# Second MLP product in pairs of output sets: half steps in turn, block sums on GpSimd, two evictions by ScalarE

## The chip, the cores and the metric

One core of a Trainium2 chip runs the whole kernel. TensorE multiplies, VectorE (DVE), ScalarE (ACT) and GpSimd (POOL) work on tiles in SBUF and, apart from GpSimd, in the PSUM banks that TensorE writes; SyncE (SP) issues nearly all DMAs. The metric is the device time of one execution in microseconds: lower is better.

## The reference, cut to what matters

```python
def reference(x, p, ...):                       # x: 1 x 1024 x 1024, float32
    h = x
    for i in range(2):                          # two layers
        hn = rmsnorm(h, norm1[i])
        ...                                     # pooling mixer and windowed attention
        h = h + concat([pool_out, attn_out]) @ w_out[i]
        hn = rmsnorm(h, norm2[i])
        h = h + square(relu(hn @ w_up[i])) @ w_down[i]     # 1024 -> 4096 -> 1024
        gate = sigmoid(rmsnorm(h, norm3[i]) @ w_gate[i])
        h = h + gate * (p[i] @ w_ple[i])
    return rmsnorm(h, final_norm)
```

Everything is float32. The change is in the two products of the MLP, above all in the second, `@ w_down`, and at its two ends.

## The kernel before, in words

**Transposed activations, split operands.** Activations lie with the features on the partitions and the 1024 positions in the columns, as eight tiles of 128 x 1024; `hf` is a half of 512 columns. Each operand of a product is split into a rounded high part and a low part (ScalarE writes the high part, DVE subtracts it to get the low one), and three matmuls of 128x512 (high x high, high x low, low x high) stand for one float32 product.

**Seven products.** Both MLP products treat a pair of 128-row weight columns, a pair of k tiles and the two column halves as 2 x 2 blocks, and take seven block products, `P1` to `P7`, for eight. A *set* is one pair of output tiles over some k positions: a position is a pair of k tiles, and a product over n positions is 3n matmuls (`products7`). The products of a set run in the order P1, P7, P6, P2, P5, P4, P3. P1, P6, P5 and P3 add up one on the other in one PSUM bank, X; P7 and P4 in Z; P2 stands alone in Y. X banks come from a pool of three ("mm"), Y and Z banks from pools of two ("s", "e"). After each product `close` reads its bank out, so the next product into the same bank has to wait for that reading.

**The weights' side** is class `Seven`: `load` brings a set's weights by SP, `sums` makes four sums of blocks on GpSimd (L280 to L287), and `make` writes one split piece per product, `u0p`/`d0p` in layer 0 and `u1p`/`d1p` in layer 1 (ScalarE L299, DVE L301). `lead` sets how far ahead: loading, sums and pieces start so many products before they are used.

**The first product (up, `Up`)** has 16 sets of four positions. ScalarE copies P1, P7 and P6 out of PSUM into `y1` and `y2` (L1131 to L1136), DVE adds P2, P5 and P4 or takes P3 with the relu (L1139 to L1154), ScalarE squares (L1157). The squared set is one *position* of the second product. `sums` (L1162) writes its seven blocks to DRAM, `x_d`: three as they are, four as differences that DVE makes into `ys` (L1172 to L1178).

**The second product (down, `Down`)** gets these blocks back: `x_back` (L1187) is one DMA of 256 KB, a high part by ScalarE (L1192) and a low part by DVE (L1194), all in one tile `wP`. Position i serves all four output pairs t. `STEPS` lists the sets as (t, first position, last): three short ones with 3, 2 and 1 positions, thirteen of four positions, and three short ones with 3, 2 and 1 at the end, so that the four output pairs run one position apart. `close` (L1205) adds every product with one DVE instruction from PSUM into the residual `acc` (L1210). When an output pair has all 16 positions, `rest` splits it into `g` (L504, L506) and squares it for the third norm (`norm3.add`, L424 on ScalarE, L426 on GpSimd).

**What sets the order.** Each engine has one queue and runs it in order; SP's queue of DMA issues too. The program is written by a planner (`Clock`): it keeps an estimate of TensorE's time, and a generator's `yield 900.0` puts the next instruction into its queue 900 ns later by that estimate. It knows no queue's real backlog. `ck.need` and `Seven.take` only see to it that a piece has been put into its queues before its product. All big tiles come from one pool of 49 buffers of 4 KB a partition.

## Time and profile before

| | us |
|---|---|
| median of 3 runs | 2370.72 (2370.68 to 2378.85) |
| the profiled execution, its own time | 2371.51 |
| its span in the trace | 2369.7 |
| TensorE busy | 2299.1 (97%) |
| DVE busy | 1711.4 (72%) |
| ScalarE busy | 1007.9 (43%) |
| GpSimd busy | 713.5 (30%) |
| matmuls | 11088 |

In layer 0 the first MLP product runs from 422.8 to 741.5 us of the span and the second from there to 1067.0; in layer 1 from 1587.2 to 1905.9 and to 2231.7. Busy shares are means over the whole program; what a change is worth is read from the places where TensorE stands still, and there from what it waited for. The granted clock of TensorE stands in the tables as a share of its full 2.4 GHz: 0.50 is 1.2 GHz.

### The profile page before, as it was taken

The page shows a single profiled execution, that of the slowest core. Times are in us where ns is not written, and L with a number is a line of the kernel's source. Part 1 is how long each engine was busy: PE and PEld are TensorE (multiplying, and loading weights), DVE is VectorE, ACT ScalarE, POOL GpSimd, SP SyncE. Part 2 cuts the span into 40 slices and gives each one's busy share as a digit, 9 for nine tenths or more (in the row PEclk, how much of TensorE's full clock was granted, in tenths as well). Part 3 has the DMA queues.
Part 4 walks back from the last instruction along what each step waited for, and adds up shares of the span by engine and source line. Part 5 has one row for each costly group of instructions (what it writes and reads, how often), then busy time and mean ns, then how long its engine had stood idle before and what let it go on. Part 6 is the DMA issues. An engine that isn't in the chain of part 4 may idle for free.

```text
span 2369.7 us, 30964 instructions
## 1 busy us (share of the span) xinstructions
PE 2299.1 (97%) x11088; PEld 1850.5 (78%) x11088; DVE 1711.4 (72%) x2888; ACT 1007.9 (43%) x2161; POOL 713.5 (30%) x562
## 2 busy tenths in 40 slices
PE   8999999999999999989999999999999989999898
PEld 6767778788887788877887767887888868888788
DVE  7555667787778888886565466677777798888845
ACT  5244533443335344444324344434433354443545
POOL 5111126323332433342221122253333233332422
PEclk9999999999999999999999999999999999999999
DMA  5011133255448555521120111333444485553214
GB/s 178 19 46 19 38 90 107 67 165 158 155 150 285 160 158 158 149 67 45 55 63 19 37 37 38 90 119 103 154 156 156 155 286 152 158 157 107 85 54 134
DMA packets 292401, 268.31 MB, mean 113 GB/s; under 512 B 12092, under 2 KB 223672, under 8 KB 292248
## 3 DMA queue, kind: packets, MB, share of 16 engines
q1 hardware_dynamic: 289656, 262.70, 36.5%
q0 software_dynamic: 2272, 3.61, 0.9%
q8 instruction: 87, 1.43, 0.2%
q14 instruction: 66, 0.54, 0.1%
q10 hardware_dynamic: 320, 0.03, 0.0%
HBM read 193.65 MB, written 72.58 MB: 112 GB/s over the span
## 4 chain that ended last, share of the span: by engine, by line
PE 46%; DVE 4%; ACT 1%; POOL 1%; DMA 1%; issue 1%; SPq 0%; DVEq 0%; ACTq 0%; POOLq 0%
PE X L535 13%; PE Z L535 7%; PE Y L535 3%; PE in L520 3%; PE in L518 3%; PE in L522 3%; PE gt L522 2%; PE gt L520 2%; PE gt L518 2%; PE s L752 1%; PE o L788 1%; DMA wP<-x_d 1%; PE e L774 1%; PE pl L520 1%; PE pl L522 1%
## 5 line engine op out<-in xcount | busy, mean ns | idle before, releaser
L535 PE MATMUL X<-wP,d1p 128*128 128x512 f32 x768 | 186.7, 393 | 15.0 <-DVE acc L1210 14.4
L535 PE MATMUL X<-wP,d0p 128*128 128x512 f32 x768 | 188.7, 396 | 12.8 <-DVE acc L1210 11.9
L535 PE MATMUL X<-xP,u0p 128*128 128x512 f32 x768 | 186.2, 394 | 3.9 <-ACT y L1131 3.9
L535 PE MATMUL X<-xP,u1p 128*128 128x512 f32 x768 | 185.8, 394 | 3.9 <-ACT y L1131 3.9
L1194 DVE TENSOR_TENSOR wP<-wP 128x512 fp32r<-128x512 f32 x224 | 183.4, 821 | 5.1 <-ACT wP L1192 5.1
L535 PEld LDWEIGHTS X<-wP,d1p 128*128 128x128 f32 x768 | 143.4, 188 | 51.0 <-ACT d1p L299 10.2
L535 PEld LDWEIGHTS X<-wP,d0p 128*128 128x128 f32 x768 | 144.6, 190 | 48.9 <-ACT d0p L299 9.1
L535 PEld LDWEIGHTS X<-xP,u0p 128*128 128x128 f32 x768 | 146.2, 191 | 35.3 <-ACT y L1131 4.7
L535 PEld LDWEIGHTS X<-xP,u1p 128*128 128x128 f32 x768 | 145.9, 190 | 35.2 <-ACT y L1131 4.8
L1157 ACT ACTIVATE y<-y 128x1024 f32<-128x1024 f32 x64 | 67.5, 1055 | 221.5 <-DVE y L1154 221.5
L1192 ACT ACTIVATE wP<-wP 128x512 fp32r<-128x512 f32 x224 | 137.9, 620 | 43.7 <-DMA wP<-x_d 43.3
L188 DVE SCALAR_TENSOR_TENSOR wl<-wr,gt,wh 128x128 fp32r<-128x128 f32 (+1 forms) x288 | 118.7, 443 | 38.5 <-ACT wh L194 38.2
L647 POOL TENSOR_TENSOR rot<-rot,s 128x512 f32<-128x512 f32 x48 | 61.5, 1284 | 277.2 <-DVE rot L645 216.2
L1210 DVE TENSOR_TENSOR acc<-acc,X 128x512 f32<-128x512 f32 x152 | 103.5, 682 | 33.7 <-PE X L535 29.9
L765 ACT ACTIVATE sm<-sm,nm 128x128 f32<-128x128 f32 (+1 forms) x192 | 84.5, 442 | 93.3 <-DVE nm L762 93.1
L194 ACT ACTIVATE wh<-wr,gt 128x128 fp32r<-128x128 f32 (+1 forms) x304 | 104.2, 396 | 0.8 <-DMA wr<-in_w_in_dram 0.7
L758 DVE CUSTOM_DVE_ANT_0 sm<-s,cst 128x128 f32<-128x128 f32 (+1 forms) x192 | 58.3, 346 | 52.0 <-PE s L752 52.0
L535 PE MATMUL Z<-xP,u1p 128*128 128x512 f32 x384 | 94.6, 394 | 0.3 <-DVE xP L1009 0.2
L535 PE MATMUL Z<-xP,u0p 128*128 128x512 f32 x384 | 94.4, 394 | 0.3 <-DVE xP L1009 0.2
L535 PE MATMUL Z<-wP,d0p 128*128 128x512 f32 x384 | 93.5, 390 | 0.0
L535 PE MATMUL Z<-wP,d1p 128*128 128x512 f32 x384 | 93.4, 389 | 0.0
L535 PEld LDWEIGHTS Z<-xP,u1p 128*128 128x128 f32 x384 | 72.9, 190 | 16.3 <-DVE xP L1009 0.5
(474 smaller groups left out, 5982.7 us busy)
## 6 DMA issues: line engine op xcount, KB each, us to landing
wP<-x_d SPq DMA_DIRECT2D x224, 256.0 KB, 2.8
x_d<-ys SPq DMA_DIRECT2D x64, 512.0 KB, 3.5
wr<-in_w_in_dram SPq DMA_DIRECT2D x40, 512.0 KB, 3.8
u0r<-in_w_up_dram SPq DMA_DIRECT2D x32, 512.0 KB, 5.3
x_d<-y SPq DMA_DIRECT2D x32, 512.0 KB, 2.8
u1r<-in_w_up_dram SPq DMA_DIRECT2D x32, 512.0 KB, 5.3
d0r<-in_w_down_dram SPq DMA_DIRECT2D x26, 512.0 KB, 5.2
d1r<-in_w_down_dram SPq DMA_DIRECT2D x26, 512.0 KB, 5.8
```

The costliest lines, as they stand in the source:

```text
L188: nc.vector.scalar_tensor_tensor(l[:, k], raw[:, k], gs[k], f(h[:, k]), op0=OP.mult, op1=OP.subtract)
L194: nc.scalar.activation(h[:, k], raw[:, k], AF.Copy, scale=gs[k])
L518: nc.tensor.matmul(p, wh, h[:, cols], start=first and i == 0, stop=False)
L520: nc.tensor.matmul(p, wh, l[:, cols], start=False, stop=False)
L522: nc.tensor.matmul(p, wl, h[:, cols], start=False, stop=last and i == n - 1)
L535: nc.tensor.matmul(p, w[:, a, i], x[:, b], start=first and i == 0 and a == b == 0, stop=i == n - 1 and a == 1, skip_group_check=not first)
L647: nc.gpsimd.tensor_tensor(a, a, tb["s"][:, hs(hf)], op=OP.mult)
L765: nc.scalar.activation(sm[:, i, hh], sm[:, i, hh], AF.Exp, bias=nm[:, j:j + 1], scale=0.125, accum_out=ml[g][:, n, 4 + h:5 + h])
L1157: nc.scalar.activation(y, y, AF.Square)
L1192: nc.scalar.activation(t[:, 0], f(t[:, 1]), AF.Copy)
L1194: nc.vector.tensor_tensor(t[:, 1], f(t[:, 1]), f(t[:, 0]), op=OP.subtract)
L1210: nc.vector.tensor_tensor(a, a, p, op=OP.add)
```

## The change

- **The sets of the second product.** `STEPS` is now (t, first position, number of positions): output pairs 2 and 3 take positions 0 and 1, then the pairs 0 and 1, then 2 and 3, and so on take four positions each, two positions further every time, and pairs 2 and 3 end with positions 14 and 15. There are 18 sets for 19; the matmuls are as many as before. The products of the first two sets, of the last two, and of the last two sets of the first product run in turn, set by set within each product: P1, P1, P7, P7 and so on.
- **Evictions.** P1 and P6 of a down set are copied by ScalarE into a tile `out`, and GpSimd adds them to `acc` 700 ns later by the planner; the other five stay on DVE.
- **The block sums** of `Up.sums` move from DVE to GpSimd, 1400 ns apart.
- **Blocks back.** `x_back` of positions 0 to 3 now starts during the last two up sets, four after each of their seven products (0, 1.4, 15 and 17.5 us after it). Later, two positions come back after each second set of a pair: one at once and one 9.5 us later.
- **Smaller ones.** The kicks of `Seven` go by a product's real length; small sets share a tile (`two`); the last two out-projection products take other PSUM banks; P5 and P4 of the last `combine` come 4500 instead of 900 ns after P6; `norm3` starts 7000 instead of 3000 ns after the last product.

```diff
-STEPS = [(3, 0, 3), (2, 0, 2), (1, 0, 1)] + [(a % 4, a, min(a + 4, 16)) for a in range(16)]
+ORDER = ("P1", "P7", "P6", "P2", "P5", "P4", "P3")
+STEPS = [(2, 0, 2), (3, 0, 2)] + [(2 * (i // 2 % 2) + i % 2, i // 2 * 2, 4) for i in range(14)]
+STEPS += [(2, 14, 2), (3, 14, 2)]
...
             ck.go(xpiece(i, "P6", T2))
-            yield 900.0
+            yield 900.0 if i < 3 else 4500.0
             ck.go(xpiece(i, "P5", T1))
...
-        outs = [(bank(f"po{L}", ("s", "e")[k // 2]), wk(ws[k % 2], range(8)), hs(k // 2)) for k in range(4)]
+        outs = [(bank(f"po{L}", ("mm", "o", "e", "e")[k]), wk(ws[k % 2], range(8)), hs(k // 2)) for k in range(4)]
...
-                sub = nc.vector.tensor_tensor
+                sub = nc.gpsimd.tensor_tensor
...
+                    if P in ("P1", "P6"):
+                        if P == "P1":
+                            self.out = blk("out")
+                        o = self.out[:, hs(n)]
+                        nc.scalar.activation(o, p, AF.Copy)
+                        ck.go(self.later(a, o))
+                        continue
                     nc.vector.tensor_tensor(a, a, p, op=OP.add)
...
+            def later(self, a, o):
+                yield 700.0
+                nc.gpsimd.tensor_tensor(a, a, o, op=OP.add)
...
-                D7.lead(7 * 12 * 225.0, 2700.0)
-                early = [(i, P) for P in ORDER for i in range(3)] + [(3, P) for P in ORDER]
-                for n, (i, P) in enumerate(early):
-                    ck.at(3200.0 + 1150.0 * n, lambda i=i, P=P: ck.go(x_back(i, P)))
+                D7.lead(8 * 12 * 225.0)
+            n = q - len(seq) + 15
+            if n > 0 and n % 2 == 0:
+                for i in range(4):
+                    ck.at((0.0, 1400.0, 15000.0, 17500.0)[i], lambda i=i, P=seq[q][1]: ck.go(x_back(i, P)))
...
-            if k >= 3 and s.a + 4 < 16:
-                ck.go(x_back(s.a + 4, P))
+            if n == 4 and t % 2 and a + 4 < 16:
+                ck.go(x_back(a + 4, P))
+                ck.at(9500.0, lambda i=a + 5, P=P: ck.go(x_back(i, P)))
...
-        norm3.start(3000.0)
+        norm3.start(7000.0)
```

Three places in the engines' queues, by the order of the built programs (layer 0; the same lines stand 20 to 31 further down in the changed file).

**GpSimd and SP at the start of the second product.** Before, GpSimd has only the weights' sums of the short sets there (`d0s`, from the raw weights `d0r`):

```order
L282 TENSOR_TENSOR d0s0_6267<-d0r1_6184 128x256
L285 TENSOR_TENSOR d0s1_6311<-d0s0_6267,d0r0_6182 128x256
L287 TENSOR_TENSOR d0s1_6311<-d0r0_6182,d0s1_6311 128x256
L280 TENSOR_TENSOR d0s0_6429<-d0r0_6365,d0r1_6367 128x128
L282 TENSOR_TENSOR d0s0_6429<-d0r1_6367 128x128
```

Now GpSimd's queue there, of which this is the end, holds sixteen instructions in a row: the block sums `ys` of the last two up sets (6280 and 6281 of position 14, 6331 and 6332 of position 15), the sums of the third down set and the adds of the first pair's P1 and P6:

```order
L1241 TENSOR_TENSOR acc6_0_6296<-acc6_0_6296,out_6318 128x512
L1193 TENSOR_TENSOR ys0_6331<-y2_6007,y1_5962 128x512
L1197 TENSOR_TENSOR ys1_6281<-y2_5986,ys0_6280 128x512
L302 TENSOR_TENSOR d0s0_6320<-d0r1_6235 128x512
L1195 TENSOR_TENSOR ys0_6331<-y1_5962 128x512
L1200 TENSOR_TENSOR ys1_6281<-y2_5986,ys1_6281 128x512
L305 TENSOR_TENSOR d0s1_6363<-d0s0_6320,d0r0_6233 128x512
L1197 TENSOR_TENSOR ys1_6332<-y2_6007,ys0_6331 128x512
L307 TENSOR_TENSOR d0s1_6363<-d0r0_6233,d0s1_6363 128x512
L1241 TENSOR_TENSOR acc5_0_6267<-acc5_0_6267,out_6294 128x512
L1200 TENSOR_TENSOR ys1_6332<-y2_6007,ys1_6332 128x512
L1241 TENSOR_TENSOR acc7_0_6298<-acc7_0_6298,out_6318 128x512
```

And SP's queue now has the writes of those sums in front of blocks of positions 2 and 3 (`x_d0_2`, `x_d0_3`) that the third set uses:

```order
L1198 DMA x_d0_15_3881<-ys0_6331 128x2x512
L1212 DMA wP5_6375<-x_d0_3_3869 128x512
L1202 DMA x_d0_14_3880<-ys1_6281 128x2x512
L1212 DMA wP4_6411<-x_d0_2_3868 128x512
L1202 DMA x_d0_15_3881<-ys1_6332 128x2x512
L1212 DMA wP4_6432<-x_d0_3_3869 128x512
L273 DMA d0r0_6443<-in_w_down_dram 128x8x128
```

What moved: eight sums went from DVE into GpSimd's queue, and the write of the last one stands ahead of the last blocks of the third set.

**ScalarE at the start of the first product.** `t1`, `t2` are the block sums of the last pair of out-projection rows, X0_3894 is the bank of the first set. Before:

```order
L1007 ACTIVATE xP7_3944<-t1_0_3940 128x512
L1007 ACTIVATE xP6_3953<-t2_0_3941 128x512
L1007 ACTIVATE xP5_3960<-t1_0_3940 128x512
L1007 ACTIVATE xP4_3968<-t2_0_3941 128x512
L1131 ACTIVATE y1_3981<-X0_3894 128x512
L1131 ACTIVATE y1_3983<-X0_3895 128x512
```

Now:

```order
L1027 ACTIVATE xP7_3944<-t1_0_3940 128x512
L1027 ACTIVATE xP6_3953<-t2_0_3941 128x512
L1152 ACTIVATE y1_3974<-X0_3894 128x512
L1152 ACTIVATE y1_3976<-X0_3895 128x512
L319 ACTIVATE u0p_3980<-u0s1_3797 128x512
L1027 ACTIVATE xP5_3985<-t1_0_3940 128x512
```

What moved: the two copies that free the X banks stand ahead of P5's and P4's high parts.

**The end of the second product.** Before, on DVE, with X0_8800 the bank of the last set and the row `acc6_0_6240<-...,X0_8800` its P1:

```order
L506 SCALAR_TENSOR_TENSOR g3_4_0L_8687<-acc4_0_6408,gt_104,g3_4_0H_8686 128x512
L301 TENSOR_TENSOR d0p_8762<-d0s0_8709,d0p_8762 128x128
L1210 TENSOR_TENSOR acc5_0_6410<-acc5_0_6410,Z0_8713 128x512
L506 SCALAR_TENSOR_TENSOR g3_5_0L_8689<-acc5_0_6410,gt_104,g3_5_0H_8688 128x512
L178 TENSOR_TENSOR wl27_8708<-wr27_8703,wh27_8707 128x1024
L301 TENSOR_TENSOR d0p_8778<-d0s1_8742,d0p_8778 128x128
L1210 TENSOR_TENSOR acc4_0_6408<-acc4_0_6408,X0_8692 128x512
L506 SCALAR_TENSOR_TENSOR g3_5_0L_8689<-acc5_0_6410,gt_104,g3_5_0H_8688 128x512
L1210 TENSOR_TENSOR acc6_0_6240<-acc6_0_6240,X0_8800 128x512
```

Now P1 and P6 of the last pair of sets (banks X0_8681 and X0_8701) are read on ScalarE:

```order
L1230 ACTIVATE out_8691<-X0_8681 128x512
L319 ACTIVATE d0p_8699<-d0r_8495 128x256
L444 ACTIVATE sqt_c0_8705<-acc2_0_6625 128x512
L1230 ACTIVATE out_8714<-X0_8701 128x512
L319 ACTIVATE d0p_8716<-d0s_8542 128x256
L319 ACTIVATE d0p_8728<-d0s_8563 128x256
L319 ACTIVATE d0p_8739<-d0r_8471 128x256
L1230 ACTIVATE out_8691<-X0_8681 128x512
L319 ACTIVATE d0p_8749<-d0r_8495 128x256
L178 ACTIVATE wh27_8697<-wr27_8693 128x1024
L1230 ACTIVATE out_8714<-X0_8701 128x512
```

What moved: the reading of P1, which stood behind four `g` and gate-weight instructions on DVE, is one of ScalarE's, with three small ones between two of them.

## Rows read from the trace of the kernel before

**Rows 1.** Waits of TensorE, whole span: total us, times, longest us

```profile
PE X L535 <- DVE acc L1210: 26.3, 19, 5.2
PE X L535 <- ACT y L1131: 7.8, 4, 3.1
PE ss_c L437 <- POOL sq_c L426: 3.5, 4, 1.2
PE Y L535 <- DVE res L1046: 1.3, 2, 0.7
```

**Rows 2.** Stretches: length, busy us (count) by engine, granted clock, DMA share, GB/s

```profile
core 0: us, PE busy (x) PEld busy (x) DVE busy (x) ACT busy (x) POOL busy (x), PEclk, DMA share, GB/s
...
441.00:447.00 6.00, 5.53 (x13) 4.38 (x14) 3.14 (x5) 4.51 (x10) 3.91 (x3) 0.50 0.00 0
470.00:741.00 271.00, 270.24 (x1192) 223.53 (x1191) 206.72 (x250) 109.43 (x178) 80.98 (x57) 1.00 0.51 163
...
741.50:781.10 39.60, 33.13 (x127) 23.77 (x126) 38.66 (x65) 21.05 (x43) 14.42 (x14) 0.96 0.90 307
783.00:1030.00 247.00, 247.00 (x1091) 204.53 (x1090) 209.97 (x273) 103.86 (x181) 79.18 (x52) 1.00 0.49 141
1030.80:1067.00 36.20, 29.88 (x119) 22.98 (x118) 32.60 (x48) 17.33 (x38) 18.46 (x16) 0.91 0.30 94
...
1906.00:1946.20 40.20, 31.66 (x127) 22.52 (x126) 38.77 (x67) 21.17 (x43) 12.22 (x12) 1.00 0.87 293
...
2196.00:2231.70 35.70, 29.23 (x119) 22.42 (x118) 32.62 (x48) 17.30 (x38) 18.45 (x16) 0.95 0.32 96
```

**Rows 3.** TensorE in order of time: start us, us, what, [idle before and its releaser]

```profile
437.61 0.73 PE L535 MATMUL Z<-xP,u0p 128*128 128x512 f32 x2 [0.22 <-DVE xP L1009]
441.47 5.49 PE L535 MATMUL X<-xP,u0p 128*128 128x512 f32 x12 [3.13 <-ACT y L1131]
...
747.66 3.88 PE L535 MATMUL X<-wP,d0p 128*128 128x512 f32 x9 [1.94 <-DVE acc L1210]
...
1060.65 1.62 PE L535 MATMUL X<-wP,d0p 128*128 128x512 f32 x3 [5.19 <-DVE acc L1210]
...
1913.33 2.32 PE L535 MATMUL X<-wP,d1p 128*128 128x512 f32 x9 [3.19 <-DVE acc L1210]
```

**Rows 4.** ScalarE in order of time at the start of the first product

```profile
438.25 1.15 ACT L1007 ACTIVATE xP<-t 128x512 fp32r<-128x512 f32 x2 [1.42 <-DVE t L1075]
...
440.83 1.07 ACT L1131 ACTIVATE y<-X 128x512 f32<-128x512 f32 x2
```

**Rows 5.** By line and shape, 470 to 1072: busy us, mean ns | idle before

```profile
L1210 DVE TENSOR_TENSOR acc<-acc,X 128x512 f32<-128x512 f32 x76 | 51.7, 682 | 17.1 <-PE X L535 15.4
...
L1175 DVE TENSOR_TENSOR ys<-y,ys 128x512 f32<-128x512 f32 x16 | 21.8, 1364 | 0.0
...
L282 POOL TENSOR_TENSOR d0s<-d0r 128x512 f32<-128x512 f32 x13 | 22.7, 1746 | 0.0
...
L1131 ACT ACTIVATE y<-X 128x512 f32<-128x512 f32 x14 | 8.4, 597 | 11.4 <-PE X L535 11.4
```

**Rows 6.** GpSimd and DVE in order of time, down sets

```profile
804.64 1.62 POOL L287 TENSOR_TENSOR d0s<-d0r,d0s 128x512 f32<-128x512 f32 x1
...
805.03 1.78 DVE L301 TENSOR_TENSOR d0p<-d0s,d0p 128x512 fp32r<-128x512 f32 x1
...
807.33 0.68 DVE L1194 TENSOR_TENSOR wP<-wP 128x512 fp32r<-128x512 f32 x1
807.93 0.68 DVE L301 TENSOR_TENSOR d0p<-d0r,d0p 128x512 fp32r<-128x512 f32 x1
...
758.19 0.41 DVE L301 TENSOR_TENSOR d0p<-d0s,d0p 128x256 fp32r<-128x256 f32 x1
```

**Rows 7.** Blocks back (tile wP): DMA issue to landing, 783 to 1030, then 725 to 783

```profile
DMA to landing us min/median/max: 2.4/2.7/5.8
...
DMA to landing us min/median/max: 3.3/5.8/7.0
```

More of the change, by code (lines that the diff above doesn't have):

```diff
@@ L269, in load, with two, part @@
                 self.raw[j].append(r)
+        def two(self, name, n, shape):
+            if n > 2:
+                return [lambda i=i: blk(f"{self.name}{name}{i}", F32, (128, *shape)) for i in range(2)]
+            b = []
+            def part(i):
+                if not b:
+                    b.append(blk(f"{self.name}{name}", F32, (128, 2, *shape)))
+                return b[0][:, i]
+            return [lambda i=i: part(i) for i in range(2)]
         def block(self, j, t, k):
@@ L1085, in layer @@
         n7 = len(sevens[L][0])
-        seq = first + [(j, P) for j in range(2, n7) for P in ("P1", "P7", "P6", "P2", "P5", "P4", "P3")]
+        seq = first + [(j, P) for j in range(2, n7 - 2) for P in ORDER]
+        seq += [(j, P) for P in ORDER for j in (n7 - 2, n7 - 1)]
         S7 = Seven(sevens[L][0], seq, f"u{L}")
```

82 lines of the change are left out of this document (43 added, 39 removed).

## The prediction

> **What bounds the kernel now.** TensorE is busy for 97% of the span, so I read the waits of TensorE first: they say how much there is to win. Four groups touch this change [Rows 1]: 26.3 us for DVE's adds into `acc`, 7.8 us for ScalarE's copies out of the X bank, 3.5 us for the third norm's squares, 1.3 us for the residual's eviction.
>
> The table of stretches says where and what it costs with all side effects. In the steady part of the second product TensorE shows 247.00 of 247.00 us busy for 1091 matmuls [Rows 2]: 0.2264 us each, so a product over four positions takes 2.72 us, one over two 1.36 us, a set of four 19.0 us. Nothing can be won there. At its start three short sets hold 126 matmuls, 28.5 us, and take 39.6 us in layer 0 and 40.2 us in layer 1 [Rows 2]: 11.1 and 11.7 us lost. At its end 117 matmuls, 26.5 us, take 36.2 and 35.7 us [Rows 2]: 9.7 and 9.2 us lost. DVE is busy for 38.66 of 39.6 us in the first and 32.60 of 36.2 us in the second [Rows 2], and TensorE's waits there name its adds: 1.94 and 3.19 us at the start, 5.19 us at the end [Rows 3]. At the start of the first product a wait of 3.13 us for ScalarE [Rows 3] is followed by a granted clock of 0.50, 1.2 GHz for 2.4 (13 matmuls in 6.0 us [Rows 2], where 2.9 would do). All these places together hold some 59 us; with all of it gone the program would take about 2312 us.
>
> **The change, part by part.** The sum goes against the profiled execution's own time, 2371.5 us, 0.8 us above the median of 2370.7.
>
> *Start of the first product.* The copies that free X stand now behind P6's high part and not behind P5's and P4's. P6's is the first of the two that begin at 438.25, so the copy can begin at about 438.9 instead of 440.83 [Rows 4]: TensorE goes on 2.0 us sooner. The bank change takes 0.65 us more (1.3 in two [Rows 1]) off the way there, but P7 then waits that much longer for DVE (it already waits 0.22 [Rows 3]), so I count it at nothing. The wait that is left is about 1.1 us. If the clock stays at 1.00, up to 3.1 us a layer come on top. Clocks fell after 1.94 us at 747.66 as the lower share of that stretch shows (0.96), and did not after 3.19 us at 1913.33 (1.00) [Rows 2, 3], so I take two thirds of it. Gain 4 a layer, **8** in all, ends 4 and 10.
>
> *Block sums on GpSimd, up sets.* When DVE takes two SBUF inputs while GpSimd works, it stops: an instruction begun at 805.03, inside a GpSimd one of 1.62 us from 804.64, takes 1.78 us for 0.68 [Rows 6]. On average of the steady part: 273 DVE instructions at a pitch of 0.60 (807.33 to 807.93 [Rows 6]) make 163.8 of 209.97 us, the other 46.2 us fall on 52 GpSimd instructions [Rows 2], 0.89 each. So four sums moved save DVE 2.4 us a set and cost it up to 3.6. DVE, busy for 206.72 of 271 us [Rows 2], goes from 14.5 to 15.7 us of 19.0 a set; GpSimd from 5.7 to 12.2. TensorE waits for neither there: **0**. Were this cover gone, it would be 1.2 us for each of 32 sets.
>
> *Steady down sets.* P1's and P6's eviction leaves DVE (2 x 0.60 saved; the instruction itself shows 682 ns [Rows 5]) and puts two adds on GpSimd (2 x 0.89 lost): 16.2 becomes 16.7 us a set. ScalarE's copy takes 597 ns [Rows 5] against 2.72 us of the product between, and ScalarE is busy for 103.86 of 247 us [Rows 2]. But blocks come back unevenly: by the planner's times, with a low part 5.9 us after its DMA, 9 of 14 low parts fall into the first set of a pair and 5 into the second. The first has then 17.9 of 19.0 us of DVE. And the blocks of the second position of a round are issued 12.2 us after a set's start and done at the earliest at 18.8, where they are used at 21.1 (their position is the fourth): 2.3 us to spare, with DVE at 94%. There are six such rounds a layer. Ends 0 and 20 us (1.7 us in each of 12); I take a quarter us each: **-3**.
>
> The Trainium skill (SBUF — State Buffer, Who interferes with whom) says that a GpSimd instruction reading SBUF and a DVE instruction with two SBUF inputs share a lock for the whole instruction, the later one blocked outright. That speaks against putting sums on GpSimd; by it a GpSimd instruction could hold DVE for its whole 1.62 us, the fuller sets would need 19.4 us of 19.0, and this term would be -5 and not -3. The single collision above agrees with it, the average of 0.89 does not reach it.
>
> *Start of the second product.* Let T0 be the end of the last up product. Two queues matter. DVE: from position 14's last P4 (T0-5.4) to the reading of the first P5, for which P3 waits, there are 39 instructions, as much as 27 of 512 columns and 14 of 256: 27 x 0.60 + 14 x 0.41 [Rows 6] = 21.9 us, T0+16.5, against P3's turn at T0+16.3. That is no loss; with some 12 GpSimd instructions at 0.89 it is 10.9. GpSimd: sixteen instructions stand in a row, eight of them block sums, that the planner puts into some 9 us. They need 1.62 to 1.75 us each ([Rows 6], [Rows 5]). From T0+3 on the fifteenth, the last block sum, ends at T0+27. SP waits with its write and holds back the last blocks of position 3 behind it; these take 3.3 to 7.0 us to land in a crowded stretch, 5.8 in the middle [Rows 7]: T0+33. ScalarE takes them in its order ahead of the third set's P1 eviction, so P6 of that set, due at T0+24.5, starts at about T0+35: 10.5 us lost; with the planner's spacing of 1.4 us and 3.3 us to land, 2.7. Both delays lie over each other. I take 8.5 us for what is still lost, nearer to the late end, because the GpSimd rows give its duration. Gain 2.6 and 3.2: **5.5**, ends -4 and 18.
>
> *End of the second product.* P1 is read by ScalarE with three products, 4.1 us, to spare; on DVE it stood behind `g` and gate weights, the 5.19 us. P5's reading still is DVE's: from the pair's start as much as 10 instructions of 512 columns and 9 of 256, 9.7 us, with eight GpSimd ones 16.8, against P3's turn at 16.3. Then the last `g` parts have to be there for the gate. I leave 2 us a layer, ends 0 and 5: gain 7.7 + 7.2, **15**. The clock, 0.91 and 0.95 there [Rows 2], comes back with it.
>
> *Third norm.* Its sums are asked for 4 us later, when the squares are there; two gate products cover that. The 3.5 us [Rows 1] go: **3.5**.
>
> *Fewer sets* (18 for 19) and the packing of small ones change no matmul: 0.
>
> Sum: 8 + 0 - 3 + 5.5 + 15 + 3.5 = 29. 2371.5 - 29 = 2342.5, and 0.8 less against the median: **2342 us**.
>
> **The rivals.**
> *The backlog does not bite.* If GpSimd keeps its pace, or the held blocks come in time, the start loses 1 us and not 8.5: 16 us more, 2326. For it: blocks now come back over 50 us and not 32. Against it: the sixteen instructions in a row.
> *DVE at its limit.* The rounds come late by 1.7 us each (17 more than forecast) and the start gains nothing (5.5): 2364. For it: 94% and 2.3 us; against it: a steady stretch with 85% and no wait at all [Rows 2].
> *Slower: ScalarE becomes the gate of the X bank.* P1's and P6's copies stand in order behind blocks that wait for their DMA, planned at 5.0 us, where the slowest took 5.8 [Rows 7]. It decides from a delay of 2.1 us on (2.72 less 0.60). With 1 us lost at both in 28 sets of four: 56 us, 2398. Against it: 2.7 us is the middle [Rows 7].
> *It does not do what it says.* Collisions give DVE back all that the moves take off it; only the end and the norm gain, 18.5 us: 2352.
>
> **How the numbers follow.** Forecast 0.54 (its own range 2331 to 2354), backlog harmless 0.16, DVE at its limit 0.18, ScalarE the gate 0.06, nothing relieved 0.06. The range, 2324 to 2364, reaches to the first two rivals, about the middle of each, and leaves out the slower one and the ends. A measurement of this kernel can tell about 0.5%, 11.9 us, from no change. Below 2358.8 lie nearly all of the forecast and of the first rival, most of the last and a quarter of the second: 0.78. Within 0.5%: the rest of the second and small parts, 0.16. Slower: 0.06.
>
> **What would show it.** Right: at the end of the second product no wait for `acc` beyond 2 us and 19 us for the last 84 matmuls plus 2; at the first product's start a wait for `y` near 1 us; at the second's start GpSimd busy without a gap for some 25 us and TensorE waiting in the third set's P6 on `out`. Wrong: a start without waits (the backlog does not count), or TensorE below its busy time in the steady sets, with waits on `wP` (rounds late) or on ScalarE's `out` (the gate).

## The result: slower by 0.8%

The changed kernel takes 2392.14 us by the median of 4 runs (2389.8 to 2392.8) against 2370.7 before; the ratio estimated from all the runs is 1.0083, 95% interval 1.0071 to 1.0095. Forecast were 2342 us, a range of 2324 to 2364, and a gain. One run of an experiment below, of 10830.3 us, was in a slow state and is left out of its median and ratio. The profiled executions span 2388.0 and 2369.7 us, 18.3 us apart, and the traces say where these lie.

The page's line of busy time, and the waits of TensorE over the whole span (total us, times, longest us), for the kernel after:

```profile
PE 2298.2 (96%) x11088; PEld 1852.8 (78%) x11088; DVE 1629.0 (68%) x2660; ACT 1032.1 (43%) x2219; POOL 1018.2 (43%) x754
```

```profile
PE Y L555 <- DVE wP L1216: 20.3, 12, 1.7
PE X L555 <- ACT out L1230: 19.6, 6, 5.7
...
PE ss_b L457 <- POOL sq_b L446: 5.1, 4, 2.3
...
PE X L555 <- DVE acc L1233: 4.6, 2, 3.6
PE pp L1476 <- DVE p_1L L522: 2.8, 1, 2.8
PE pp L1476 <- DVE p_0L L522: 2.6, 1, 2.6
PE X L555 <- ACT y L1152: 2.2, 2, 1.1
```

Against [rows 1]: the wait for `acc` shrank from 26.3 us to 4.6, as the change means it to. In its place stand two others: 20.3 us for the low parts of blocks (`wP`, 1.2 before) and 19.6 for ScalarE's copies (`out`, which did not exist). DVE is less busy (68% for 72%), GpSimd more (43% for 30%), and the program is slower.

To place the loss I count the second product from its own rhythm. Where nothing waits, the trace has 19.04 us from the P2 of one set to the P2 of the next, 84 matmuls, 0.2267 us each. By that a layer's 1344 matmuls take 304.6 us. What a stretch takes beyond its matmuls is its loss. The start runs to the P2 of the fourth set before, of the fifth after; the rounds from there to the P2 of the last full set (after: of the last pair); the end to the first gate product. All in us, layer 0 and layer 1; the first product is given by its length, the gate as the stage from its first matmul to the next layer's out-projection (layer 0) or to the end (layer 1):

| | first product | start | rounds | end | gate and on |
|---|---|---|---|---|---|
| before | 318.7 / 318.7 | 11.2 / 11.9 | 0 / 0 | 9.7 / 9.2 | 432.3 / 138.1 |
| after | 318.0 / 317.0 | 16.9 / 18.4 | 12.0 / 11.9 | 0.3 / 0.3 | 431.6 / 141.6 |
| after less before, both | -2.5 | +12.2 | +23.9 | -18.3 | +2.8 |

The sum is +18.1, what the spans differ by within 0.2.

Stretches of the kernel after (length, busy us and count by engine, granted clock, DMA share, GB/s), against [rows 2]:

```profile
441.00:447.00 6.00, 4.86 (x20) 3.64 (x18) 6.00 (x5) 5.60 (x10) 5.27 (x4) 0.78 0.00 0
470.00:740.80 270.80, 270.80 (x1196) 224.24 (x1195) 183.06 (x197) 112.45 (x184) 170.33 (x116) 1.00 0.50 162
...
740.80:796.00 55.20, 42.52 (x170) 33.25 (x169) 43.56 (x55) 22.63 (x45) 33.22 (x22) 0.91 0.72 247
804.00:1044.40 240.40, 230.24 (x1009) 188.64 (x1008) 188.40 (x232) 108.33 (x199) 111.36 (x73) 1.00 0.46 140
1044.40:1074.60 30.20, 30.14 (x133) 24.64 (x132) 25.63 (x35) 18.16 (x37) 24.79 (x20) 1.00 0.35 105
```

The last line is the end of the second product: 30.14 of 30.20 us busy at a clock of 1.00. The end no longer waits. The line above it is the steady part, which before had no wait at all; it now has six in layer 0, and in layer 1 as many. In the start of the second product (the third line) DVE is busy for 43.56 of 55.20 us, where it was for 38.66 of 39.60: it is relieved, and yet the start loses more. TensorE in order of time there, and the second of GpSimd's instructions:

```profile
757.50 2.93 PE L555 MATMUL X<-wP,d0p 128*128 128x512 f32 x6 [5.47 <-ACT out L1230]
762.79 1.66 PE L555 MATMUL X<-wP,d0p 128*128 128x512 f32 x6 [2.36 <-ACT out L1230]
...
770.75 7.31 PE L555 MATMUL X<-wP,d0p 128*128 128x512 f32 x24 [3.58 <-DVE acc L1233]
...
782.06 3.01 PE L555 MATMUL X<-wP,d0p 128*128 128x512 f32 x12 [1.28 <-ACT out L1230]
```

```profile
750.10 1.29 POOL L1241 TENSOR_TENSOR acc<-acc,out 128x512 f32<-128x512 f32 x1 [5.82 <-DMA acc<-h_d]
```

**One round.** TensorE, ScalarE, GpSimd and DVE in order of time (start us, us, what, and in brackets the idle time before it and who ended that), 854 to 869 us of the kernel after:

```profile
863.07 2.43 PE L555 MATMUL Y<-wP,d0p 128*128 128x512 f32 x10
867.19 0.73 PE L555 MATMUL Y<-wP,d0p 128*128 128x512 f32 x2 [1.69 <-DVE wP L1216]
```

```profile
851.85 0.64 ACT L1214 ACTIVATE wP<-wP 128x512 fp32r<-128x512 f32 x1
857.83 0.60 ACT L1230 ACTIVATE out<-X 128x512 f32<-128x512 f32 x1 [5.35 <-PE X L555]
858.33 0.62 ACT L319 ACTIVATE d0p<-d0s 128x512 fp32r<-128x512 f32 x1
858.85 1.14 ACT L1214 ACTIVATE wP<-wP 128x512 fp32r<-128x512 f32 x2
...
860.41 0.62 ACT L1214 ACTIVATE wP<-wP 128x512 fp32r<-128x512 f32 x1
863.27 0.60 ACT L1230 ACTIVATE out<-X 128x512 f32<-128x512 f32 x1 [2.24 <-PE X L555]
```

```profile
858.51 1.30 POOL L1241 TENSOR_TENSOR acc<-acc,out 128x512 f32<-128x512 f32 x1 [5.78 <-ACT out L1230]
859.76 1.75 POOL L302 TENSOR_TENSOR d0s<-d0r 128x512 f32<-128x512 f32 x1
861.58 1.63 POOL L305 TENSOR_TENSOR d0s<-d0s,d0r 128x512 f32<-128x512 f32 x1
```

```profile
860.28 1.78 DVE L1216 TENSOR_TENSOR wP<-wP 128x512 fp32r<-128x512 f32 x1
861.98 0.68 DVE L1233 TENSOR_TENSOR acc<-acc,Z 128x512 f32<-128x512 f32 x1
...
865.39 1.75 DVE L1216 TENSOR_TENSOR wP<-wP 128x512 fp32r<-128x512 f32 x1
```

Read it from TensorE back. The last two matmuls of the P2 product begin when DVE's low part of 865.39 ends, at 867.14. By the order of the blocks in both queues it belongs to P2's block of the round's second position, whose high part is ScalarE's of 860.41. DVE's low parts take 1.75 and 1.78 us there, for 0.68, while GpSimd works from 858.51 on without a gap. GpSimd does that because it stood for 5.78 us behind an add whose operand ScalarE had not yet copied. ScalarE stood for 5.35 us behind the same copy: the P1 product in X was still running, and the high parts of the next blocks stand behind the copy in ScalarE's order. Their blocks have landed: the two at 858.85 run without a wait for a DMA. So the two instructions that took the eviction off DVE hold up the blocks on the one engine and bunch the collisions on the other; whether it takes both, the experiments ask. The six periods of a layer are alike, and a wait of 1.69 us costs 2.0: the set with the wait takes 21.02 us, the next 19.04.

The Trainium skill (PSUM — Partial Sum Buffer, Engine vs sequencer instructions) calls the queues of ScalarE and GpSimd strict FIFO. The trace agrees: 5.35 and 5.78 us idle with work behind.

### The profile page after: what moved, and what is told of

It reads as the page before. It is cut to its first block, busy times and chain, and to the rows that moved or that the text cites. A ratio compares the mean times of both kernels' runs of the same rounds, so it can differ in the third digit from the quotient of the medians.

```text
span 2388.0 us, 30872 instructions
## 1 busy us (share of the span) xinstructions
PE 2298.2 (96%) x11088; PEld 1852.8 (78%) x11088; DVE 1629.0 (68%) x2660; ACT 1032.1 (43%) x2219; POOL 1018.2 (43%) x754
## 4 chain that ended last, share of the span: by engine, by line
PE 78%; DVE 10%; issue 4%; POOL 3%; ACT 3%; DMA 2%; SPq 0%; DVEq 0%; ACTq 0%; POOLq 0%
PE X L555 25%; PE Z L555 12%; PE in L540 5%; PE in L538 5%; PE in L542 5%; PE Y L555 5%; PE gt L542 2%; PE gt L540 2%; PE gt L538 2%; DVE wP L1216 2%; PE s L772 2%; PE o L808 2%; PE e L794 1%; POOL res L1045 1%; DMA wP<-x_d 1%
## 5 line engine op out<-in xcount | busy, mean ns | idle before, releaser
L1216 DVE TENSOR_TENSOR wP<-wP 128x512 fp32r<-128x512 f32 x224 | 210.8, 949 | 6.5 <-ACT wP L1214 6.4
L555 PE MATMUL X<-wP,d1p 128*128 128x512 f32 x768 | 187.4, 396 | 11.6 <-ACT out L1230 10.5
L555 PEld LDWEIGHTS X<-wP,d1p 128*128 128x128 f32 x768 | 146.3, 191 | 45.1 <-ACT out L1230 12.2
L1241 POOL TENSOR_TENSOR acc<-acc,out 128x512 f32<-128x512 f32 x72 | 108.8, 1513 | 110.5 <-ACT out L1230 70.2
L1230 ACT ACTIVATE out<-X 128x512 f32<-128x512 f32 x72 | 42.8, 594 | 256.5 <-PE X L555 256.5
L1193 POOL TENSOR_TENSOR ys<-y,y 128x512 f32<-128x512 f32 x32 | 42.2, 1318 | 211.8 <-ACT y L1178 211.8
```

Of the source, the lines that this page charges most:

```text
L555: nc.tensor.matmul(p, w[:, a, i], x[:, b], start=first and i == 0 and a == b == 0, stop=i == n - 1 and a == 1, skip_group_check=not first)
L1216: nc.vector.tensor_tensor(t[:, 1], f(t[:, 1]), f(t[:, 0]), op=OP.subtract)
L1241: nc.gpsimd.tensor_tensor(a, a, o, op=OP.add)
```

## The experiments

Each is the changed kernel with the edit shown, unless it says otherwise. "Start", "rounds" and "end" are those of the table, each from one trace. Ratios are to the kernel before, run again beside each (medians 2371.7 to 2372.5 us).

Two cautions on these numbers. Four traces of kernels that hardly differ up to the end of the start (the changed one and those with the second position's blocks sooner, with its high parts sooner and with the row sums later) lose 16.9 to 18.7 us there in layer 0 and 17.5 to 19.8 in layer 1, so a difference of under 2 us in the start says nothing. And where the late block of a round is P1's or P7's and not P2's, the wait of the first round falls ahead of the P2 that ends the start and is counted there, with 0.6 to 1.5 us: so in the runs with all evictions by DVE and in the one with GpSimd's add later.

**The parts undone, and the margin.** Block sums back on DVE:

```diff
-                sub = nc.gpsimd.tensor_tensor
+                sub = nc.vector.tensor_tensor
...
-                yield 1400.0
+                yield 1000.0
```

> The changed kernel with one part undone: the block sums of the first product's sets are made by DVE again, at their old spacing; everything else stays. The second product now takes 333.9 and 335.3 us in the two layers, where its 1344 matmuls at 0.2264 us would take 304.3; about 17 and 18.5 us of the excess lie in its start, 10.2 in its six rounds. Theory (backlog): the sums queue up on GpSimd, hold SP's writes and with them the blocks, and ScalarE's eviction stands behind those; then the start gets back 10 us or more a layer, and the wait of 5.7 us for out at the start falls under 2. Rival (the eviction's place on ScalarE, whoever makes the sums): the start keeps its 17 us within 3, perhaps loses more since DVE is fuller. The waits in the rounds, which lie after the last of these sums, stay at 12 of 1.7 us by both.

Measured: 2386.09 us (ratio to before 1.0064, 1.0048 to 1.0081). The start loses 13.3 / 13.3 us instead of 16.9 / 18.4, the first product gets 0.9 / 1.9 us longer, the rounds stay at 12.1. The backlog on GpSimd is a part of the start's loss, 3.6 and 5.1 us: less than the theory's 10, more than the rival's 3, and the first wait for `out` stays at 4.9. The first product gets longer by a wait for `y` in its third set, 1.06 us a layer, which the kernel before has too (shown below); the rest is the spread of its start.

P1 and P6 evicted by DVE again:

```diff
-                    if P in ("P1", "P6"):
...
-                        nc.scalar.activation(o, p, AF.Copy)
-                        ck.go(self.later(a, o))
-                        continue
```

> The changed kernel with one part undone: P1 and P6 of the second product are added into acc by DVE straight out of the bank again; no copies by ScalarE, no adds on GpSimd. Theory (collisions): the low parts of a round's second position are late because the adds on GpSimd hold DVE up in the burst just ahead; without them the 12 waits of 1.7 us fall under 0.5 and about 15 us come back. Rival (the margin alone): two DVE adds a set take the place of what the collisions cost, and the waits stay above 1.2 us. At the start the waits for out, 19.6 us, go by construction; if blocks are late there for their own reasons, TensorE waits for wP or acc instead and the start keeps over 10 us of its loss a layer; if the copies' place on ScalarE is the cause, the loss falls under 8 a layer.

Measured: 2360.28 us (0.9955, 0.994 to 0.997), faster than before. The rounds' loss falls from 12 to 4.7 us a layer, the collision theory's number. But the wait of 1.69 us at P2 is gone altogether, and one of 0.48 us at P1 came in its place:

```profile
853.92 0.73 PE L555 MATMUL X<-wP,d0p 128*128 128x512 f32 x2 [0.50 <-DVE wP L1216]
```

GpSimd's sums of weights no longer stand behind an add and run some 8 us sooner against TensorE, from 846.48 to 853.31, and now it is P1's low part that takes 1.77 us beside them. ScalarE's copies went too, so the run doesn't say which of the two engines held up P2's block. The start still loses 15.4 / 14.9 (14.6 / 14.1 without the first round's wait); the waits only changed their name to `acc`. The gate got shorter by 4.3 and 4.8 us (below).

Second position's blocks sooner:

```diff
-                ck.at(9500.0, lambda i=a + 5, P=P: ck.go(x_back(i, P)))
+                ck.at(6000.0, lambda i=a + 5, P=P: ck.go(x_back(i, P)))
```

> The changed kernel with one number changed: in each round the blocks of the second position are called back 6.0 us after the first position's, not 9.5. Theory (a margin of 2.3 us that the collisions eat, with 1.7 us to spare on the other side): 3.5 us sooner is enough, the 12 waits of 1.7 us vanish, and 20 us come back; about 2372 us. Rival (DVE's throughput is the limit in a round's first set): the low parts stand in DVE's queue whenever the blocks come, the waits stay above 1 us each and the time stays within 6 us of 2392. The start of the second product is not touched: 17 us lost by both.

Measured: 2369.16 us (0.999, 0.998 to 0.9999). All 12 waits are gone, the rounds lose 0.4 us a layer. DVE has the room: what is late is the blocks' way to it. The time is 3 us below the theory's 2372.

The loads of `acc` ahead of the crowd:

```diff
+            if q in (len(seq) - 6, len(seq) - 4):
+                for m in ((4, 5) if q == len(seq) - 6 else (6, 7)):
+                    acc[m] = blk(f"acc{m}_{L}")
+                    nc.sync.dma_start(out=acc[m], in_=h_d[m])
```

> The changed kernel with the four loads of acc that the start of the second product needs moved ahead, to the last six and four products of the first product, so that they are issued ahead of the crowd of block writes and reads. Theory (late acc): GpSimd's first add waits 5.8 us for its load, all that GpSimd does afterwards is late by that, and DVE's first adds wait for it as well; then the start gets back 4 to 8 us a layer. Rival (the eviction's place on ScalarE behind blocks that wait for their DMA): the first waits of TensorE for out, 5.5 and 5.7 us, stay within 1 us, and the start gains under 2 us a layer.

Measured: 2386.04 us (1.006, 1.0045 to 1.0075). The start loses 12.8 / 14.5, so 4.1 and 3.9 less: the lower edge of what the late load was expected to cost. The rival is right on the first wait for `out`, which stays (5.6 and 5.8).

**Which engine makes the rounds late.** GpSimd's add behind the block sums:

```diff
             def later(self, a, o):
-                yield 700.0
+                yield 5000.0
```

> The changed kernel with one number changed: GpSimd's add of an evicted product into acc is put 5.0 us after the copy in the order, not 0.7, so that it stands behind the block sums of the weights and these no longer wait behind it. Theory (collisions): in the changed kernel GpSimd stands still for 5.8 us behind such an add, and then works off one add, three sums and one more add back to back, just where DVE makes the low parts of the second position; these take 1.75 us instead of 0.68. With the sums out of the way the 12 waits of 1.7 us fall to 0.6 or less, and 13 us or more come back. Rival (ScalarE's order: its copy out of the X bank stands ahead of the blocks and waits 5.4 and 2.2 us for TensorE): GpSimd's order changes nothing of that, and the waits stay between 1.3 and 1.8 us.

Measured: 2381.11 us (1.0032, 1.0019 to 1.0044). The waits fall to 0.82 us, more than the rival allowed and less than the theory asked for; the rounds lose 5.8 us a layer, 7.3 and 6.9 with the wait that is counted in the start. The number hides what happened. The wait at P2 is gone in all twelve rounds, though ScalarE's copy still stands for 5.48 us ahead of the blocks' high parts. In its place an earlier product, P7, waits:

```profile
860.19 0.73 PE L555 MATMUL Z<-wP,d0p 128*128 128x512 f32 x2 [0.83 <-DVE wP L1216]
```

GpSimd's row of sums was not taken away but moved ahead, to 850.38 to 859.59, and now holds up the low part of P7's block. So ScalarE's order alone does not make P2's block late; it takes GpSimd's row at that place as well.

The second position's high parts on ScalarE 2.0 us sooner by the planner, and with them, 0.9 us behind each, their low parts on DVE; the loads stay:

```diff
-                ck.at(9500.0, lambda i=a + 5, P=P: ck.go(x_back(i, P)))
+                ck.at(9500.0, lambda i=a + 5, P=P: ck.go(x_back(i, P, 3000.0)))
...
-            yield 5000.0
+            yield due
```

> The changed kernel with one number changed: the high-part copy of a second position's block is planned 3.0 us after its issue, not 5.0; the issue itself stays 9.5 us behind the first position's. So in ScalarE's order two more of these copies stand ahead of the copy out of the X bank, and the loads are not any earlier. Theory (ScalarE's order): the high parts no longer wait behind an eviction whose product is still running; they are made as soon as the block has landed (2.7 us at the middle), and the 12 waits of 1.7 us fall to 0.5 or less; 14 us or more come back. Rival (collisions alone): GpSimd's burst lies where it lay, and the waits stay above 1.2 us.

Measured: 2371.06 us (0.9991, 0.9981 to 1.0001), and no wait in the rounds (loss 0.1 and 0.3). The blocks are issued at the same place as in the changed kernel, and GpSimd's burst lies where it lay. ScalarE in order of time, 854 to 860 us of this run:

```profile
854.48 1.14 ACT L1214 ACTIVATE wP<-wP 128x512 fp32r<-128x512 f32 x2
858.53 0.60 ACT L1230 ACTIVATE out<-X 128x512 f32<-128x512 f32 x1 [2.92 <-PE X L555]
```

Counted in the layer's order, one high part more is done before the copy begins to wait (the text above says two). P2's high part still stands behind the copy, but 1.6 us sooner against TensorE, and its low part, which now passes two other instructions in DVE's order, 4.2 us sooner. So the chain needs both: GpSimd's row (the run before this one) and the late place of the blocks (this one). Either of the two relieved takes the whole wait at P2 away. How much of the late place is ScalarE's order and how much DVE's, the edit does not separate, since it moved both; no run does.

**The start of the first product.** Row sums of the second norm later:

```diff
-        norm2.start(14000.0, slack=3000.0)
+        norm2.start(17000.0, slack=3000.0)
```

> The changed kernel with one number changed: the row sums of the second norm stand four matmuls' worth of products later in TensorE's order at the start of the first product (17.0 us, not 14.0). In the changed kernel the wait for y there fell from 3.1 to 1.1 us as it should, but TensorE then waits 2.3 us for the last square that GpSimd adds (about 0.4 before), and the clock falls twice. Theory (the stall went to the next late thing): with the sums later by about 1.6 us of matmuls, that wait falls from 2.3 to about 0.7, and the first product gets shorter by 1.5 to 4 us a layer, the more if the clock stays up. Rival (the squares are not the reason, the clock falls from the waits for y and for the last blocks alone): the first product stays at 318.0 and 317.0 us within 0.7.

Measured: 2389.56 us (1.0069, 1.0053 to 1.0085). The wait for the squares is 1.23 us in layer 0 and stays 2.29 in layer 1; the first product takes 315.65 and 316.74 us. The kernel after and the six runs here with the same start of that product have 317.0 to 318.3 and 317.0 to 317.9. That is a gain of 1.3 to 2.7 us in layer 0 and of 0.2 to 1.1 in layer 1: the direction is the theory's. The last version below has the same edit, and its first two sets lose as much as here, 11.0 and 12.1 us beyond their 168 matmuls; the fifteen runs without the edit lose 12.4 to 13.7 and 12.3 to 13.3. So layer 0's gain is there twice; layer 1's is too small to tell.

**Parts alone, on the kernel before.** Only the block sums by GpSimd:

```diff
-                sub = nc.vector.tensor_tensor
+                sub = nc.gpsimd.tensor_tensor
...
-                yield 1000.0
+                yield 1400.0
```

> One part of the change done alone, on the kernel before: the block sums of the first product's sets by GpSimd, 1.4 us apart. From the run that undid this part (start of the second product 3.4 and 4.8 us shorter, first product 0.9 and 1.9 us longer): if the parts are independent of each other, the start here gets longer by 3 to 5 us a layer through the sums that queue on GpSimd, the first product shorter by 1 to 2; about 2375 us. Rival (before, DVE is busy for 38.7 of 39.6 us of that start, so whatever is taken off it helps): the start gets shorter by 2 us or more a layer; 2364 us or less.

Measured: 2372.46 us (1.0004, 0.9994 to 1.0013). The start loses 13.8 / 13.3 (2.6 and 1.4 more), the first product is 1.0 and 1.1 us shorter: the wait for `y` in its third set is gone. Nothing that can be measured in the whole.

Only P1 and P6 by ScalarE and GpSimd:

```diff
+                    if P in ("P1", "P6"):
...
+                        nc.scalar.activation(o, p, AF.Copy)
+                        ck.go(self.later(a, o))
+                        continue
```

> One part of the change done alone, on the kernel before: P1 and P6 of the second product are copied out of the bank by ScalarE and added by GpSimd; the blocks come back as before, one position a set. Theory (it takes the copies and the rounds of two positions together to be late): no waits over 0.5 us in the steady sets of the second product, which stay at full speed; the whole within 6 us of 2371. Rival (the copies cost wherever they stand): waits for wP or out of 0.5 us or more in each of the sets of four positions, 13 a layer; 2384 us or more.

Measured: 2373.8 us (1.0009, 1.0 to 1.0018). No loss in the steady sets, as the theory has it: with one position called back in each set, the copies hurt nobody there. The start loses 15.9 / 15.7 (4.7 and 3.8 more). The end loses 9.4 in both layers, as before: the copies alone do nothing for it.

**The start of the second product.** The last two sets of the first product one after the other:

```diff
-        seq = first + [(j, P) for j in range(2, n7 - 2) for P in ORDER]
-        seq += [(j, P) for P in ORDER for j in (n7 - 2, n7 - 1)]
+        seq = first + [(j, P) for j in range(2, n7) for P in ORDER]
```

> The changed kernel with one part undone: the last two sets of the first product run one after the other again and not in turn; the blocks are called back at the same products. Theory (the pair makes the crowd: two positions' sums, eight on GpSimd, and 14 block writes fall together at the very end): the first of the two positions is written 19 us sooner, SP and GpSimd are half as full at the start of the second product, and its loss of 17 and 18.5 us falls by 4 us or more a layer. Rival (the crowd is the second product's own: two positions in turn need an eviction every 1.4 us and blocks as fast): the start keeps its loss within 2 us. The rounds stay at 12 waits of 1.7 us by both.

Measured: 2386.78 us (1.0062, 1.0047 to 1.0077). The start loses 13.1 / 13.1, 3.8 and 5.3 less; but the first product is 2.3 us longer in both layers, with a wait of 1.69 us for X at its last turn. The pair buys its place at the end of one product with a crowd at the start of the next.

Both shifts of work undone in the changed kernel (evictions and block sums by DVE, the first two diffs together):

> The changed kernel with both shifts of work undone: the block sums of the first product and the evictions of P1 and P6 are DVE's again; the new order of the sets, the rounds of two positions and the early blocks stay. Up to the second product's seventh tenth (the first four of its sets' middle products) the start loses 16.9 and 18.4 us in the changed kernel, 11.2 and 11.9 before; with the sums undone alone 13.3, with the evictions undone alone 15.4 and 14.9. Theory (GpSimd's new work is all of the start's loss, the pairs themselves neither gain nor lose there): 10 to 12.5 us. Rival (the pairs cost by themselves): 14 us or more. The rounds lose about 4.7 us a layer, as with the evictions undone alone; the end loses nothing; 2355 us by the theory, 2361 by the rival.

Measured: 2360.15 us by the median of three runs (0.9951, 0.9935 to 0.9968); the start loses 13.4 / 12.4, or 12.6 / 11.6 without the first round's wait. That is about the theory's 10 to 12.5, though the time is nearer to the rival's 2361. The same two shifts alone on the kernel before, the two diffs for it together:

> The kernel before with both shifts of work and nothing else of the change: block sums by GpSimd, P1 and P6 by ScalarE and GpSimd; sets and blocks in their old order. Alone, the sums made the start of the second product lose 13.8 and 13.3 us (before 11.2 and 11.9), the copies 15.9 and 15.7. Theory (what GpSimd is given adds up there, and the new order has no part in it): 17.5 to 19.5 us; no loss in the steady sets, 9 to 10 at the end; 2376 to 2380 us. Rival (they overlap, one delay hides the other): 16 us or less, 2374 us or less; then the new order is to blame for one to two us of the changed kernel's start.

Measured: 2378.69 us (1.0022, 1.0012 to 1.0032); the start loses 18.1 / 19.6, the steady sets nothing, the end 9.4. Waits of TensorE in this run:

```profile
PE X L535 <- DVE acc L1218: 13.8, 8, 4.9
...
PE X L535 <- DVE wP L1195: 5.4, 7, 1.7
```

So the shifts alone make the start as bad as in the changed kernel: 6.9 and 7.7 us more than before, where the two alone add up to 7.3 and 5.2. The new order with pairs takes 1.2 us of it back in both layers; in the kernel without the shifts it costs 1.4 and gives back 0.3 (13.4 / 12.4 less the first round's wait, against 11.2 / 11.9). Both are within the spread of the traces. So nearly all that the start lost against the kernel before comes with the work shifted to ScalarE and GpSimd.

**Towards a faster version.** Evictions by DVE, blocks at 6.0 us and loads of `acc` early, by the diffs above; then the same with the block sums by DVE (the bracket with 121.9 us in the second text is a slip and says nothing):

> Three edits of this study together: evictions of P1 and P6 by DVE again, the second position's blocks 6.0 us after the first, and the four loads of acc ahead of the crowd. With evictions by DVE alone the program took 2360.3 us by its median, with 12 waits of 0.48 us in the rounds and DVE standing 3.1 us for a load of acc at the start. If the three add up: the rounds give 5.8 us, the start 3 to 5 us a layer: 2346 us. If the start is bound by DVE's own work (busy for 23.6 of 24 us behind the wait for acc) and not by the load: 2354 us, and the waits of TensorE for acc there stay above 7 us a layer.

> Evictions of P1 and P6 by DVE, the second position's blocks at 6.0 us, the loads of acc early (together 2359.8 us by its median, start 121.9 us for layer 0's first 40 us excepted nothing else late) and, new here, the block sums by DVE again. Theory (at the start GpSimd's twelve sums back to back stretch DVE's low parts from 0.41 to 1.5 us, so DVE is late with the eviction that frees X; wait 4.65 us): without them that wait falls under 2 and the second product gets 3 us or more shorter a layer, the first at most 1.5 us longer; 2354 us. Rival (DVE has no room for eight sums there): the wait for acc stays over 4 us, and the time is 2360 us or more.

Measured: 2359.84 (0.9941, 0.9925 to 0.9957) and 2355.04 us (0.9927, 0.991 to 0.9943). The first misses its 2346: the start loses 13.1 / 13.5, bound by DVE itself (busy for 24.00 of the 24 us from 756 on), and the rounds still 3.9, now in 0.33 us waits for DVE's `acc` adds. The second's start loses 13.9 / 11.5; the wait for `acc` stays, 5.5 and 6.4 us, so there the rival is right, though the time came out near the theory's.

Copies by ScalarE in the steady sets only, with the other edits:

```diff
-                    if P in ("P1", "P6"):
+                    if P in ("P1", "P6") and 4 <= self.j < len(STEPS) - 4:
```

> A version put together from what the runs showed: copies of P1 and P6 by ScalarE only in the steady sets (neither in the first four nor in the last four), the second position's blocks 6.0 us after the first, the loads of acc early, block sums by DVE, and the row sums of the second norm four matmul groups later. If each piece gives what it gave alone: the start loses 11.5 to 14 us (as in the run with the same edits and all evictions by DVE), the rounds at most 0.5 instead of 4.2, the end nothing, the two gate stages stay 4 us shorter than in the changed kernel; 2347 us. If the copies hold the blocks up even so: rounds that lose 4 us or more, 2356 us.

Measured: 2346.03 us (0.9891, 0.9876 to 0.9906): faster than both kernels by more than 1%. The start loses 10.6 / 10.9, the rounds 1.4, the end nothing. The rounds' 1.4 are more than the 0.5 expected, the start's loss is less than the 11.5 to 14. TensorE's longest group of waits on the two products in this run:

```profile
PE X L555 <- DVE acc L1232: 16.6, 9, 6.4
```

What is left lies at the start: one wait of 6.4 us in each layer, for DVE's adds into `acc` again.

## Why the prediction was wrong

By the terms of its sum (gain plus; 29 forecast, -18.1 found):

- **Steady down sets: -3 forecast, -23.9 found.** This is most of the miss. The end of the range, 20 us, "1.7 us in each of 12", has the size of the wait that came, but that is luck: its reason was DVE at 94% with 2.3 us to spare, and DVE is busy for 15.2 us in a round's one set and 16.0 in the other, 76 to 80%, less than before. The step that failed is the margin of the blocks. It was counted for P1's block alone, by the planner's times (5.9 us from a block's issue to its low part) and DVE's work. P1's block is there about 2 us early, much as counted. P2's, three products later, is the late one: its high part stands on ScalarE behind the copy of P1, which waits 5.35 us in order for a product that still runs, and its low part on DVE in the row of GpSimd's work that the same copy let pile up, 4.36 us behind the high part. I had ScalarE's order in a rival, but the other way round (copies behind blocks that wait for their DMA); here blocks wait behind copies.
- **Start of the second product: +5.5 forecast, -12.2 found.** (The two gains named there, 2.6 and 3.2, add up to 5.8.) The chain I described shows: sixteen GpSimd instructions from 742.99 to 772.8, blocks held back on SP, and P6's copy behind them. But I had one long wait, in the third set's P6, and that one is 1.28 us; the loss begins in the first pair: 5.47 us at 757.50, 2.36 at 762.79, then 3.58 for `acc`. I had counted DVE's relief and set the backlog against it; the runs show that the copies alone cost the start 4.7 / 3.8 us, the sums alone 2.6 / 1.4, both 6.9 / 7.7. And two things I did not see at all: loads of `acc` that land late (about 4 us a layer; the second of the sixteen waits 5.82 us for one), and the paired end of the first product (about 4 to 5). These don't add up to one cause: taking away one of them exposes the next.
- **End of the second product: +15 forecast, +18.3 found.** The number came, but not by the step that I gave it. I had credited the eviction of P1 by ScalarE. With the copies and the old order the end still loses 9.4 us a layer; with the new order and DVE's evictions, in five runs, it loses 0.0, where the changed kernel loses 0.3. What took the wait away is the new order of the last sets; which part of it, no run separates.
- **Start of the first product: +8 forecast, about +0.3 found.** The first product as a whole got 2.5 us shorter, but only 0.3 of it lies here: its first two sets lose 13.0 us in both layers before, 13.3 and 12.4 after. The wait for `y` fell to 1.07 us, as forecast (about 1.1). But the next thing was late:

```profile
439.50 4.61 PE L555 MATMUL X<-xP,u0p 128*128 128x512 f32 x12 [1.07 <-ACT y L1152]
...
448.39 1.87 PE L457 MATMUL ss_b<-one,sq_b 128*128 128x1 f32 x8 [2.29 <-POOL sq_b L446]
```

  I did not ask when the squares would be there. Their four adds end at 448.33 where they ended at 448.91, so TensorE, 2 us sooner, waits for them. The clock, at 0.50 in 441 to 447 before, is 0.78 there after and not 1.00.
- **Block sums on GpSimd in the up sets: 0 forecast, +2.1 found.** I had read that TensorE waits for neither engine there. Before, it waits once in each layer, in the third set:

```profile
480.23 3.01 PE L535 MATMUL X<-xP,u0p 128*128 128x512 f32 x12 [0.76 <-ACT y L1131]
```

  The copy stands on ScalarE behind a square that waits for DVE, and DVE has the sums in front. It costs 1.06 us a layer. All six kernels with the sums on DVE have this wait, the eleven with the sums on GpSimd do not. The cost was overrated too: I feared up to 1.2 us more of DVE a set. DVE is busy for 183.06 us of 270.8 (before 206.52): 197 instructions at 0.60 leave 64.9 us for 116 GpSimd instructions, 0.56 each and not 0.89.
- **Third norm: +3.5 forecast, -2.8 found.** `ss_c` no longer waits, but the transposes of the next stage do:

```profile
1086.75 0.66 PE L1476 MATMUL pp<-cst,pr 128*128 128x128 f32 x4 [2.59 <-DVE p_0L L522]
1087.24 2.06 PE L457 MATMUL ss_c<-one,sq_c 128*128 128x1 f32 x16
```

  With P1 and P6 evicted by DVE this wait is 0.14 us (0.42 in layer 1) and the gate's stage 4.3 and 4.8 us shorter; the last version, whose copies stop four sets before the end, has 0.14 and 0.41. So it comes with the copies of the last sets. By the traces the row of eight squares on GpSimd, 13.3 us in both, begins 4.07 us ahead of the first gate product and not 6.50, since ScalarE's squares come later, and DVE's last parts fall into it and end 2.4 us later too. That last step is read from the traces; no run took it apart.

The chances put 0.06 on slower, for one mechanism. The place it names (ScalarE's order against the blocks) was right, its direction and size were not. Of the signs of being right, no wait for `acc` at the end and a wait for `y` near 1 us both came, in a program that got slower: each sign saw one wait go and none saw what took its place.

## What to carry to other kernels

Before an eviction is moved to another engine, look at what stands behind it in that engine's order at the moment when the product is not done yet: a copy that waits for TensorE holds everything behind it, however little the engine is busy. When a stall is taken away, ask for each of the next three things on TensorE's queue when they are ready. And take work off an engine only where it is the bound: copies by ScalarE and GpSimd in the steady sets, with blocks called early, are part of the version that is 1.1% faster than the kernel before; in the crowded start and at the end DVE does better alone. When a wait gets smaller by an edit, look whether it is the same wait: twice here it was gone, and another block's had come.

## What the hardware showed

DVE's add out of a PSUM bank is not slowed by GpSimd, its work on two SBUF tiles is. In the rows on one round, DVE's add at 861.98 takes 0.68 us, between low parts of 1.78 and 1.75. From 740 to 1080 us of the kernel after, 37 such adds fall into GpSimd's busy time and take 0.67 to 0.69 us, as do the 28 that meet none of it; of the blocks' low parts the 19 that fall into it take 1.16 to 1.78 us, the 62 that meet none 0.68 to 0.69. The Trainium skill (SBUF — State Buffer, Who interferes with whom) says that a DVE instruction with at most one SBUF input, outside its two-port modes, does not contend with GpSimd; the trace agrees, for the add into `acc` has one. I had cited the neighbouring sentence, on two inputs, and not this one. It speaks against the change: an eviction that takes DVE 0.60 us and was not disturbed in any of these rows is traded for a GpSimd add that costs DVE, as an estimate from the averages, 0.56 to 0.67 us (188.40 less 232 x 0.60, over 73, is 0.67 in the steady down sets; 0.56 is the up sets' above).

A wait of 1.69 us costs TensorE 2.0 us, and one of 0.48 costs 0.8 (rounds that lose 4.7 us a layer with six waits of 0.48 to 0.50): about 0.3 us is lost beyond what the row shows.
